# Gate and up products of a feed-forward layer by one level of Strassen's algorithm, with the down product in a stage of its own

## The chip, the core and the metric

The kernel runs on one core of a Trainium2 chip. The core has a matrix engine (TensorE, "PE" in the profile, its weight loads "PEld"), three engines for elementwise work (VectorE "DVE", ScalarE "ACT", GpSimd "POOL") and an engine that issues transfers between DRAM and the on-chip memory SBUF (SyncE, "SP"). PE writes its sums into PSUM, a small memory of eight banks. Each engine works through its own list of instructions in order and waits on semaphores for the others. The metric is the device time of one execution in microseconds (us). The kernel before was timed three times: median 2945.67 us, from 2942.64 to 2949.52.

## The reference, cut to what matters

A layer of a recurrent decoder is computed for 2112 tokens (64 sample tokens and 2048 prompt tokens), width 1024. A mixer with two kinds of recurrent heads comes first, then a residual and a LayerNorm give `x`. The part that matters here follows, with 2816 hidden features:

```python
hid = jax.nn.silu(x @ w_ffn_gate) * (x @ w_ffn_up)      # 1024 -> 2816, twice
f   = hid @ w_ffn_down                                  # 2816 -> 1024
y   = layer_norm(2 ** 0.25 * x + f, ln2_g, ln2_b)
```

All inputs are float32. The kernel computes each product of two float32 matrices by three matrix products: an operand `a` is split into a rounded part `h` and a rest `l = a - h` (the type `fp32r`), and `a b` is taken as `h_a h_b + h_a l_b + l_a h_b`.

## The kernel before, in words

The program has four stages, one after the other on the one core: the GLA heads, the GDN heads, the output projection with the first LayerNorm (`phase_out`), and the feed-forward part (`phase_ffn`). Tokens are handled in 17 units: unit 0 is the 64 sample tokens, units 1 to 16 are 128 prompt tokens each. The instructions of each engine are put in their order by a scheduler when the program is built; the order is fixed then, and within an engine nothing overtakes.

`phase_out` ends each unit in `project` (L1015) with the LayerNorm of `x` (`layer_norm`, L965), stores `x` to DRAM (`x1_d`, L1050), transposes it on PE (tiles `px`, L1056) and stores the transposed tiles as `x1T_d` (L1059).

`phase_ffn` (L1079) runs over three blocks of 704, 640 and 768 tokens (`fblocks`). For each block `load_x1` (L1089) brings in the transposed `x` as eight tiles of 128 features and splits each into `xh` (ACT, L1096) and `xl` (DVE, L128). Then it goes through the 22 groups of 128 hidden features `f`, taken one and then three at a time (`groups`). For each `f`:

- `load_gu` (L1101) loads a tile of gate weights and one of up weights, 128 by 1024 each; POOL casts the `h` part (L1107), DVE subtracts for the `l` part (L128).
- For each half of the block's tokens there are 24 matmuls into a PSUM tile `g` (gate) and 24 into a tile `u` (up), at L1144 to L1146. ACT applies SiLU to `g`, DVE multiplies with `u` (tile `sg`), and the result is split into `hh` (ACT, L1151) and `hl` (DVE). It stays in SBUF.
- `load_d` (L1112) loads and splits the down weights of this `f`.

After each group of `f`, the down products of all units of the block follow (L1169 to L1171, PSUM tile `dn`), and DVE adds their sums to the tile `y` in SBUF (L128, and L1173 for the first group). After the last group of a block comes the second LayerNorm and the store of the result.

`vtt` is an elementwise operation of two tensors on DVE (recorded as L128), `ptt` the same on POOL (recorded as L131). All transfers of this part, loads and stores, are issued by SP in one queue.

Of the kernel before, what the change touches and what calls it, by code (L numbers as in the profile page):

```python
# [9 lines left out]
F32 = mybir.dt.float32  # L10
# [8 lines left out]
D = 1024  # L19
# [4 lines left out]
DFF = 2816  # L24
# [76 lines left out]
def hybrid_layer(ctx: ExitStack, tc: tile.TileContext, I, O):  # L101
# [25 lines left out]
    def vtt(out, a, b, op):  # L127
        nc.vector.tensor_tensor(out, a, b, op=op)  # L128
# [19 lines left out]
    fblocks = [(0, 704, range(0, 6)), (704, 640, range(6, 11)), (1344, 768, range(11, 17))]  # L148
    x1T_d = [dram.tile([8, 128, T], F32, name=f"x1T_{i}") for i, (_, T, _) in enumerate(fblocks)]
# [836 lines left out]
    def phase_out(stack, main, rest):  # L986
# [28 lines left out]
        def project(u, gts):  # L1015
# [35 lines left out]
            fb = [i for i, f in enumerate(fblocks) if u in f[2]][0]  # L1051
            off = u0 - fblocks[fb][0]
            for i in range(2):
                pt = pmt("px").rearrange("p (h c) -> p h c", h=4)
                for h in range(4):
# [3 lines left out]
                ST.dma_start(out=x1T_d[fb][4 * i:4 * i + 4, :, off:off + C].rearrange("k p t -> p k t"),  # L1059
                             in_=t[:, :, :C])  # L1060
# [18 lines left out]
    def phase_ffn(stack):  # L1079
        pa = stack.enter_context(tc.tile_pool(reuse_waits=RW, name="pa", bufs=2))  # L1080
        NF = DFF // 128
        groups = [range(max(g, 0), g + 3) for g in range(NF % 3 - 3, NF, 3)]

        def split(pool, tag, bufs, shape):
            h = pool.tile(shape, F32R, name=tag + "h", tag=tag + "h", bufs=bufs)
            l = pool.tile(shape, F32R, name=tag + "l", tag=tag + "l", bufs=bufs)
            return h, l

        def load_x1(ib):  # L1089
            T = fblocks[ib][1]  # L1090
            xs = []
            for k in range(8):
                raw = pa.tile([128, 768], F32, name="xr")
                nc.sync.dma_start(out=raw[:, :T], in_=x1T_d[ib][k])
                h, l = split(pa, "x", 9, [128, 768])
                nc.scalar.copy(h[:, :T], raw[:, :T])  # L1096
                vtt(l[:, :T], raw[:, :T], h[:, :T].bitcast(F32), TT.subtract)
                xs.append((h, l))
            return xs

        def load_gu(f):  # L1101
            ws = []
            for n in ("w_gate", "w_upf"):
                raw = pa.tile([128, 8, 128], F32, name="wr")
                nc.sync.dma_start(out=raw, in_=I[n][:, 128 * f:128 * f + 128].rearrange("(k p) c -> p k c", p=128))
                h, l = split(pa, "w", 3, [128, 8, 128])
# [155 lines left out]
```

## Time and profile before

| | us |
|---|---|
| three timed runs, median (range) | 2945.67 (2942.64 to 2949.52) |
| the profiled execution, its own time | 2946.43 |
| span of that execution in the trace | 2944.4 |
| PE busy in the span | 2821.6 (96%) |
| DVE, ACT, POOL busy | 1425.6, 822.6, 515.6 |
| first matmul of the feed-forward part | starts at 1389.37 |
| mean granted PE clock | 0.974 of full speed |

A group's row in the profile reads: line, engine, operation, the program's names of output and inputs, their shapes, the count; then its busy time and the mean of one in ns; then the idle time of the engine before these instructions and what ended it. A row of the timeline reads: start in us, duration in us, engine, line, operation. Matmuls overlap: the next one starts before the end of the last, so that what a matmul costs is the distance from one start to the next and not its duration. A row of the windows gives for a stretch of time its length, the busy time of PE, PEld, DVE, ACT and POOL with the number of instructions, the granted PE clock, the busy share of the transfer engines and the rate in GB/s.

### The profile page before, as it was taken

Reading aid. Unit: us, or ns where it says so; the run is one execution under the profiler, and the core shown is the slowest. Engines: PE = TensorE matmul, PEld = TensorE weight load, DVE = VectorE, ACT = ScalarE, POOL = GpSimd, SP = SyncE. Lnnn points to the kernel's source line nnn. Section 1 sums busy time; section 2 is a strip of 40 time slices with the busy share of each in tenths; the row PEclk is TensorE's granted clock in tenths of the full one; section 3 lists DMA queues with packets and bytes.
Section 4 is the critical chain, followed back from the end, with each engine's and each line's share of the span. In section 5 each row is a group of like instructions: output and inputs, shape, how many; then the busy total and the mean of one; then the engine's idle time right before and its main releaser. Section 6 shows DMA issues by size and latency. Waiting matters only on the chain.

```text
span 2944.4 us, 43629 instructions
## 1 busy us (share of the span) xinstructions
PE 2821.6 (96%) x17686; PEld 2564.2 (87%) x17686; DVE 1425.6 (48%) x2428; ACT 822.6 (28%) x1852; POOL 515.6 (18%) x742
## 2 busy tenths in 40 slices
PE   7899996989998899999999999999999999999997
PEld 6799995878986788887999999999999999999996
DVE  4444453588897544445433333463333373333334
ACT  4243344376675433333211111111111121111111
POOL 2111111343343021111100000130010010000002
PEclk9899997799999999999999999999999999999998
DMA  5211134221213333334522222342222252222211
GB/s 152 62 59 37 51 99 68 71 69 37 67 49 85 122 123 101 115 101 150 182 65 70 67 65 65 103 156 77 78 73 79 79 170 65 64 62 62 64 44 45
DMA packets 291747, 246.62 MB, mean 84 GB/s; under 512 B 40672, under 2 KB 250896, under 8 KB 291536
## 3 DMA queue, kind: packets, MB, share of 16 engines
q1 hardware_dynamic: 289456, 243.64, 27.6%
q8 instruction: 141, 2.31, 0.3%
q14 instruction: 70, 0.57, 0.1%
q10 hardware_dynamic: 2080, 0.10, 0.0%
HBM read 201.03 MB, written 42.67 MB: 83 GB/s over the span
## 4 chain that ended last, share of the span: by engine, by line
PE 85%; DMA 5%; DVE 4%; ACT 2%; issue 2%; POOL 1%; SPq 0%; POOLq 0%; ACTq 0%; DVEq 0%
PE dn L1170 6%; PE dn L1171 6%; PE dn L1169 6%; PE u L1145 6%; PE u L1146 6%; PE u L1144 6%; PE g L1146 6%; PE g L1145 6%; PE g L1144 6%; PE g L205 3%; PE g L206 3%; PE g L207 3%; PE g L212 3%; PE g L213 3%; PE g L214 3%; PE pw L214 2%
## 5 line engine op out<-in xcount | busy, mean ns | idle before, releaser
L1107 POOL CAST wh<-wr 128x1024 fp32r<-128x1024 f32 x132 | 142.0, 1076 | 1289.0 <-PE g L1145 1096.7
L1144 PE MATMUL g<-xh,wh 128*128 128x352 f32 (+2 forms) x1056 | 340.5, 323 | 1.9 <-ACT xh L1096 1.9
L1145 PE MATMUL g<-xl,wh 128*128 128x352 f32 (+2 forms) x1056 | 341.0, 323 | 1.0 <-DVE xl L128 1.0
L1146 PE MATMUL g<-xh,wl 128*128 128x352 f32 (+2 forms) x1056 | 340.4, 323 | 0.0
L1146 PE MATMUL u<-xh,wl 128*128 128x352 f32 (+2 forms) x1056 | 340.1, 322 | 0.0
L1145 PE MATMUL u<-xl,wh 128*128 128x352 f32 (+2 forms) x1056 | 340.0, 322 | 0.0
L1144 PE MATMUL u<-xh,wh 128*128 128x352 f32 (+2 forms) x1056 | 340.0, 322 | 0.0
L1169 PE MATMUL dn<-dh,hh 128*128 128x512 f32 (+1 forms) x748 | 291.0, 390 | 2.5 <-ACT dh L1116 2.5
L1170 PE MATMUL dn<-dl,hh 128*128 128x512 f32 (+1 forms) x748 | 291.8, 390 | 0.0
L1171 PE MATMUL dn<-dh,hl 128*128 128x512 f32 (+1 forms) x748 | 291.2, 390 | 0.0
L128 DVE TENSOR_TENSOR sg<-sg,u 128x352 f32<-128x352 f32 (+2 forms) x132 | 68.7, 521 | 414.8 <-PE u L1146 413.1
L128 DVE TENSOR_TENSOR y<-y,dn 128x512 f32<-128x512 f32 (+1 forms) x238 | 162.6, 684 | 215.6 <-PE dn L1171 215.5
L128 DVE TENSOR_TENSOR wl<-wr,wh 128x1024 fp32r<-128x1024 f32 x132 | 169.2, 1282 | 123.5 <-POOL wh L1107 123.5
L225 DVE SCALAR_TENSOR_TENSOR cv<-hb,cw,cv 128x256 f32<-128x256 f32 x288 | 150.6, 531 | 112.5 <-ACT cv L223 107.7
L1144 PEld LDWEIGHTS g<-xh,wh 128*128 128x128 f32 x1056 | 198.5, 188 | 4.2 <-ACT xh L1096 2.6
L1145 PEld LDWEIGHTS g<-xl,wh 128*128 128x128 f32 x1056 | 198.6, 188 | 3.5 <-DVE xl L128 1.9
L1151 ACT CAST hh<-sg 128x352 fp32r<-128x352 f32 (+2 forms) x132 | 64.2, 487 | 490.6 <-DVE sg L128 490.5
L1146 PEld LDWEIGHTS g<-xh,wl 128*128 128x128 f32 x1056 | 198.9, 188 | 0.4
L1144 PEld LDWEIGHTS u<-xh,wh 128*128 128x128 f32 x1056 | 198.4, 188 | 0.3
L1145 PEld LDWEIGHTS u<-xl,wh 128*128 128x128 f32 x1056 | 198.3, 188 | 0.4
L1146 PEld LDWEIGHTS u<-xh,wl 128*128 128x128 f32 x1056 | 198.3, 188 | 0.1
L1116 ACT CAST dh<-dr 128x1024 fp32r<-128x1024 f32 x66 | 67.3, 1050 | 446.7 <-PE dn L1171 402.2
(321 smaller groups left out, 6274.3 us busy)
## 6 DMA issues: line engine op xcount, KB each, us to landing
wr<-in_w_gate SPq DMA_DIRECT2D x66, 512.0 KB, 3.8
wr<-in_w_upf SPq DMA_DIRECT2D x66, 512.0 KB, 3.7
dr<-in_w_down SPq DMA_DIRECT2D x66, 512.0 KB, 4.0
xraw<-in_xT SPq DMA_DIRECT2D x84, 256.0 KB, 3.2
on<-on SPq DMA_DIRECT2D x48, 256.0 KB, 3.6
wraw<-in_w_in SPq DMA_DIRECT2D x20, 512.0 KB, 4.0
xt<-in_x SPq DMA_DIRECT2D x16, 512.0 KB, 4.0
x<-xt SPq DMA_DIRECT2D x16, 512.0 KB, 3.6
```

Of the source, the lines that this page charges most:

```text
L128: nc.vector.tensor_tensor(out, a, b, op=op)
L205: nc.tensor.matmul(out, lhsT=wh[:, k, cs], rhs=xs[0][k], start=(k == 0), stop=False)
L206: nc.tensor.matmul(out, lhsT=wh[:, k, cs], rhs=xs[1][k], start=False, stop=False)
L214: nc.tensor.matmul(out, lhsT=xs[1][k][:, ts], rhs=wh[:, k, :], start=False, stop=(k == 7))
L225: nc.vector.scalar_tensor_tensor(dst, hb[:, i:i + 256], cw[:, f, i:i + 1], dst, op0=TT.mult, op1=TT.add)
L1107: nc.gpsimd.tensor_copy(h, raw)
L1144: nc.tensor.matmul(ps[:, :N], lhsT=h[:, k, :], rhs=xs[k][0][:, ts], start=(k == 0), stop=False)
L1145: nc.tensor.matmul(ps[:, :N], lhsT=h[:, k, :], rhs=xs[k][1][:, ts], start=False, stop=False)
L1146: nc.tensor.matmul(ps[:, :N], lhsT=l[:, k, :], rhs=xs[k][0][:, ts], start=False, stop=(k == 7))
L1169: nc.tensor.matmul(ps[:C], lhsT=hh[:, ts], rhs=wh[:, sl], start=first, stop=False)
L1170: nc.tensor.matmul(ps[:C], lhsT=hh[:, ts], rhs=wl[:, sl], start=False, stop=False)
L1171: nc.tensor.matmul(ps[:C], lhsT=hl[:, ts], rhs=wh[:, sl], start=False, stop=last)
```

## The change

Only the feed-forward part and what feeds it are changed.

**Gate and up together, seven products for eight.** The gate and up weights of one `f` are taken as one matrix of 256 outputs, the features of `x` in two halves of 512, and the tokens of a block in two halves of 352 (three equal blocks of 704). Written in these halves, gate and up are a 2 by 2 by 2 block product: eight block products of 12 matmuls each. One level of Strassen's algorithm (in Winograd's form) makes it seven, called by the right-hand operand: `11`, `S2`, `12`, `S1`, `S3`, `S4`, `22`. It needs four sums of halves of `x` per block (`sums`, on POOL; stored to DRAM in `xS_d` for blocks 1 and 2 and loaded again), four sums of quarters of the weights for each `f` in each block (`load_gu`, on POOL, in place of the casts that POOL did; the casts are ACT's now), and seven additions of the products for each `f` (on DVE, with one operand in PSUM). Each of the seven weight operands and seven `x` operands is split into `h` and `l` on ACT and DVE (`part`). A block product takes, for each of four tiles of 128 features, three matmuls with 352 tokens: 12 matmuls; one `f` has 84.

**The down product by itself.** SiLU times up is no longer split and kept, but stored to DRAM (`hid_d`) and loaded again after all three blocks are done. The down product then runs over five groups of units (4, 4, 3, 3, 3); the sums over all 22 `f` stay in the eight PSUM banks, and the down weights are loaded and split once per group, five times in all (three times before).

**Layout.** The weights come in an order that makes each load one contiguous piece per partition (`w_gu`, `w_dn`).

```diff
-    fblocks = [(0, 704, range(0, 6)), (704, 640, range(6, 11)), (1344, 768, range(11, 17))]
...
+    FT, FN = 704, 352
...
+    xS_d = [dram.tile([4, 4, 128, FN], F32, name=f"xS_{i}") for i in range(1, 3)]
+    hid_d = [dram.tile([128, NTOK], F32, name=f"hid_{f}") for f in range(DFF // 128)]
...
+        def part(pool, tag, bufs, shape, raw, N):
...
+            nc.scalar.copy(h[:, :N], raw)
+            vtt(l[:, :N], raw, h[:, :N].bitcast(F32), TT.subtract)
             return h, l
+        XO = ("11", "S2", "12", "S1", "S3", "S4", "22")
...
+        def raw_x():
+            return pa.tile([128, FN], F32, name="xr", bufs=8)
...
+        def sums(ib, k):
+            r = {n: load_raw(ib, n, k) for n in ("11", "21", "22", "12")}
+            r["S3"], r["S2"], r["S4"] = raw_x(), raw_x(), raw_x()
+            ptt(r["S3"], r["11"], r["21"], TT.subtract)
+            ptt(r["21"], r["21"], r["22"], TT.add)
+            r["S1"] = r["21"]
+            ptt(r["S2"], r["S1"], r["11"], TT.subtract)
+            ptt(r["S4"], r["12"], r["S2"], TT.subtract)
+            return r
         def load_x1(ib):
...
+            if ib == 0:
+                for k in range(4):
+                    r = sums(0, k)
+                    for n in XO:
+                        xs[n][k] = part(pa, "x", 28, [128, FN], r[n], FN)
+                return xs
+            for n in XO:
+                for k in range(4):
...
+                    xs[n][k] = part(pa, "x", 28, [128, FN], raw, FN)
...
+        x_first = load_x1(0)
+        yield
+        pw = stack.enter_context(tc.tile_pool(reuse_waits=RW, name="pw", bufs=2, side="right"))
...
+        psp = stack.enter_context(tc.tile_pool(reuse_waits=RW, name="psp", bufs=6, space=PSUM))
         def load_gu(f):
...
+            raw = pw.tile([128, 4, 512], F32, name="wr")
+            nc.sync.dma_start(out=raw, in_=I["w_gu"][f])
+            g1, g2, u2, u1 = (raw[:, i, :] for i in range(4))
+            t3, t2, t4 = (pw.tile([128, 512], F32, name="wt", bufs=3) for _ in range(3))
+            ptt(t3, u2, u1, TT.subtract)
+            ptt(u1, u1, g1, TT.subtract)
+            ptt(t2, u2, u1, TT.subtract)
+            ptt(t4, g2, t2, TT.subtract)
+            return {n: part(pw, "w", 9, [128, 512], r, 512)
+                    for n, r in zip(XO, (g1, t2, g2, u1, t3, u2, t4))}
...
+        for ib in range(3):
+            xs = load_x1(ib) if ib else x_first
+            for f in range(NF):
+                ws = load_gu(f)
+                def prod(n):
+                    (h, l), x = ws[n], xs[n]
+                    ps = psp.tile([128, 512], F32, name="p", tag="p")[:, :FN]
+                    for k in range(4):
...
+                g1, v, w, h1, h2 = (tmp() for _ in range(5))
+                nc.scalar.copy(g1, prod("11"))
+                vtt(v, g1, prod("S2"), TT.add)
+                vtt(g1, g1, prod("12"), TT.add)
+                act(g1, g1, AF.Silu)
+                vtt(w, v, prod("S1"), TT.add)
+                p = prod("S3")
+                vtt(v, v, p, TT.add)
+                vtt(h2, w, p, TT.add)
+                vtt(h1, w, prod("S4"), TT.add)
+                ptt(h1, h1, g1, TT.mult)
+                vtt(v, v, prod("22"), TT.add)
+                act(v, v, AF.Silu)
+                ptt(h2, h2, v, TT.mult)
+                for i, t in enumerate((h1, h2)):
...
+                    ST.dma_start(out=hid_d[f][:, t0:t0 + FN], in_=t)
+                if f == 10 and ib < 2:
+                    store_sums(ib + 1)
...
+        for nu in (4, 4, 3, 3, 3):
...
+            for f in range(NF):
+                if f % 2 == 0:
+                    raw = pw.tile([128, 4, 512], F32, name="wr")
+                    nc.sync.dma_start(out=raw, in_=I["w_dn"][f // 2])
+                wd = [part(pw, "w", 9, [128, 512], raw[:, 2 * (f % 2) + i, :], 512) for i in range(2)]
+                hr = p4.tile([128, 512], F32, name="hr")
+                nc.sync.dma_start(out=hr[:, :T], in_=hid_d[f][:, c0:c0 + T])
+                hh, hl = part(p4, "h", 3, [128, 512], hr[:, :T], T)
...
                     for u in us:
...
+            for u in us:
...
```

The scheduler gives the changed program the order that it now has. Up to the last projection of `phase_out` all engines have the same rows as before. Three places differ.

The first place is PE where the feed-forward part begins. `px` are the transposes of the last unit after its first LayerNorm. Before, the last projections (`pw`) are followed at once by gate and up products:

```order
L1146 MATMUL g_14875<-xh_14794,wl_14843 128x352
L1144 MATMUL g_14875<-xh_14800,wh_14842 128x352
L1145 MATMUL g_14875<-xl_14801,wh_14842 128x352
L1146 MATMUL g_14875<-xh_14800,wl_14843 128x352
L1146 MATMUL g_14930<-xh_14794,wl_14843 128x352
```

Now they are followed by the transposes, and then by the first product (`p_15045`, product `11` of the first `f`):

```order
L216 MATMUL pw_14761<-o1l_11567,oh_14729 128x512
L217 MATMUL pw_14761<-o1h_11590,ol_14730 128x512
L215 MATMUL pw_14761<-o1h_11590,oh_14729 128x512
L216 MATMUL pw_14761<-o1l_11591,oh_14729 128x512
L217 MATMUL pw_14761<-o1h_11590,ol_14730 128x512
L1057 MATMUL px_14797<-ident_60,xt_14733 128x128 x4
L1057 MATMUL px_14805<-ident_60,xt_14733 128x128 x4
L1179 MATMUL p_15045<-xh_14833,wh_15012 128x352
```

So the transposes of the last unit, which stood 44 matmuls behind the first gate product, now stand ahead of all products.

The second place is DVE within the gate and up products of one `f`. Before, in the third block (`sg` is the product with the up sums `u` in PSUM; `wl`, `hl` have both inputs in SBUF):

```order
L128 TENSOR_TENSOR wl_23858<-wr_23855,wh_23857 128x1024
L128 TENSOR_TENSOR sg_23663<-sg_23663,u_23638 128x384
L128 TENSOR_TENSOR hl_23612<-sg_23663,hh_23611 128x384
L128 TENSOR_TENSOR wl_23864<-wr_23861,wh_23863 128x1024
L128 TENSOR_TENSOR sg_23718<-sg_23718,u_23693 128x384
L128 TENSOR_TENSOR hl_23612<-sg_23718,hh_23611 128x384
```

Now, in the first block (`p` are products in PSUM, `t` their running sums, `wt` sums of weight quarters):

```order
L128 TENSOR_TENSOR wl_16340<-wt_16329,wh_16339 128x512
L128 TENSOR_TENSOR wl_16344<-wr_16326,wh_16343 128x512
L128 TENSOR_TENSOR t_16217<-t_16216,p_16235 128x352
L128 TENSOR_TENSOR wl_16348<-wr_16326,wh_16347 128x512
L128 TENSOR_TENSOR t_16216<-t_16216,p_16249 128x352
L128 TENSOR_TENSOR wl_16352<-wt_16328,wh_16351 128x512
L128 TENSOR_TENSOR t_16218<-t_16217,p_16264 128x352
L128 TENSOR_TENSOR wl_16356<-wr_16326,wh_16355 128x512
L128 TENSOR_TENSOR t_16217<-t_16217,p_16278 128x352
L128 TENSOR_TENSOR t_16220<-t_16218,p_16278 128x352
L128 TENSOR_TENSOR wl_16360<-wt_16330,wh_16359 128x512
L128 TENSOR_TENSOR t_16219<-t_16218,p_16293 128x352
```

Six instructions per `f` have become fourteen, and subtractions of weights for the next `f` alternate with additions that wait for the products of this one.

The third place is POOL in the same stretch. Before it had two casts per `f` and nothing else:

```order
L1107 CAST wh_15713<-wr_15711 128x1024
L1107 CAST wh_15719<-wr_15717 128x1024
L1107 CAST wh_15843<-wr_15841 128x1024
L1107 CAST wh_15849<-wr_15847 128x1024
L1107 CAST wh_16105<-wr_16103 128x1024
```

Now it has six operations of two tensors per `f`; in the first four `f` of blocks 0 and 1 the sums for the next block (`xr`) stand between them:

```order
L131 TENSOR_TENSOR t_15043<-t_15043,t_15040 128x352
L131 TENSOR_TENSOR t_15044<-t_15044,t_15041 128x352
L131 TENSOR_TENSOR wt_15446<-wr_15444 128x512
L131 TENSOR_TENSOR xr_16647<-xr_16639,xr_16641 128x352
L131 TENSOR_TENSOR wr_15444<-wr_15444 128x512
L131 TENSOR_TENSOR xr_16641<-xr_16641,xr_16643 128x352
L131 TENSOR_TENSOR xr_16648<-xr_16641,xr_16639 128x352
L131 TENSOR_TENSOR wt_15447<-wr_15444 128x512
L131 TENSOR_TENSOR xr_16649<-xr_16645,xr_16648 128x352
L131 TENSOR_TENSOR wt_15448<-wr_15444,wt_15447 128x512
```

A row such as `wt_15446<-wr_15444` reads two quarters of the same tile; the casts of the weights went from POOL to ACT.

More of the change, by code (lines that the diff above doesn't have):

```diff
@@ L1087, in split @@
             return h, l
-        def load_x1(ib):
[L1090 to L1098, printed above, removed]
-            return xs
@@ new lines, in store_sums @@
+        def store_sums(ib):
+            for k in range(4):
+                r = sums(ib, k)
+                for n in range(4):
+                    ST.dma_start(out=xS_d[ib - 1][n, k], in_=r[f"S{n + 1}"])
+        x_first = load_x1(0)
+        yield
+        pw = stack.enter_context(tc.tile_pool(reuse_waits=RW, name="pw", bufs=2, side="right"))
+        p4 = stack.enter_context(tc.tile_pool(reuse_waits=RW, name="p4", bufs=2, side="right"))
+        psp = stack.enter_context(tc.tile_pool(reuse_waits=RW, name="psp", bufs=6, space=PSUM))
@@ new lines, in phase_ffn @@
+        nc.sync.dma_start(out=lng, in_=I["ln"][2:3, :].to_broadcast([128, D]))
+        nc.sync.dma_start(out=lnb, in_=I["ln"][3:4, :].to_broadcast([128, D]))
+        n = 0
+        for nu in (4, 4, 3, 3, 3):
+            us = range(n, n + nu)
+            n += nu
+            c0, T = units[us[0]][0], sum(units[u][1] for u in us)
+            ps = {}
+            for u in us:
+                for i in range(2):
+                    ps[u, i] = (psg.tile([128, 512], F32, name="g", tag="g") if u == us[0] else
+                                psp.tile([128, 512], F32, name="p", tag="p"))
+            ys = {}
+            for f in range(NF):
[6 more added lines that the diff above has]
+                hh, hl = part(p4, "h", 3, [128, 512], hr[:, :T], T)
+                if f == 0:
@@ L1154, in phase_ffn @@
                     for u in us:
-                        ys[u] = p4.tile([128, D], F32, name="y", bufs=6)
+                        ys[u] = p4.tile([128, D], F32, name="y", bufs=5)
                         nc.sync.dma_start(out=ys[u][:units[u][1]], in_=x1_d[u])
-                    if ib == 0:
-                        nc.sync.dma_start(out=lng, in_=I["ln"][2:3, :].to_broadcast([128, D]))
-                        nc.sync.dma_start(out=lnb, in_=I["ln"][3:4, :].to_broadcast([128, D]))
                 for u in us:
@@ L1163, in phase_ffn @@
                     for i in range(2):
[L1164 to L1179 removed]
+                        p = ps[u, i][:C]
+                        nc.tensor.matmul(p, lhsT=hh[:, ts], rhs=wd[i][0], start=f == 0, stop=False)
+                        nc.tensor.matmul(p, lhsT=hh[:, ts], rhs=wd[i][1], start=False, stop=False)
+                        nc.tensor.matmul(p, lhsT=hl[:, ts], rhs=wd[i][0], start=False, stop=f == NF - 1)
+            for u in us:
+                u0, C = units[u]
+                for i in range(2):
+                    sl = slice(512 * i, 512 * i + 512)
+                    nc.vector.scalar_tensor_tensor(ys[u][:C, sl], ys[u][:C, sl], ALPHA, ps[u, i][:C],
+                                                   op0=TT.mult, op1=TT.add)
+                layer_norm(p4, ys[u], C, lng, lnb, spare=u < 16)
+                ST.dma_start(out=O["y"][u0:u0 + C, :], in_=ys[u][:C])
         yield
@@ L1224, in lay_out @@
     cst, msk = make_consts()
+    quads = lambda n, d: g(n)[512 * d:512 * d + 512].reshape(4, 128, 22, 128).transpose(2, 1, 0, 3)
     one, zero = np.ones(4, np.float32), np.zeros(4, np.float32)
```

102 lines of the change are left out of this document (31 added, 71 removed).

## Prediction

> **What bounds the kernel now.** I read the page first: busy times, and the span in 40 slices of 73.6 us.
>
> ```profile
> span 2944.4 us, 43629 instructions
> PE 2821.6 (96%) x17686; PEld 2564.2 (87%) x17686; DVE 1425.6 (48%) x2428; ACT 822.6 (28%) x1852; POOL 515.6 (18%) x742
> PE   7899996989998899999999999999999999999997
> PEclk9899997799999999999999999999999999999998
> ```
>
> The reader is to see that from slice 19 on, where the feed-forward part lies, PE is full and its clock is too. The windows give the ends of that part and a stretch within it:
>
> ```profile
> 1389.40:1416.00 26.60, 21.20 (x117) 19.07 (x115) 14.39 (x19) 7.25 (x12) 6.66 (x5) 0.94 0.85 244
> 1520.00:1620.00 100.00, 100.00 (x564) 92.48 (x563) 34.84 (x47) 11.62 (x21) 10.46 (x10) 1.00 0.23 69
> 2915.00:2944.00 29.00, 10.75 (x48) 8.58 (x46) 20.12 (x23) 3.03 (x3) 14.20 (x11) 0.74 0.24 94
> ```
>
> Within it DVE works a third of the time, ACT and POOL a tenth, the transfers a quarter: PE alone is the bound. So the part costs what its matmuls cost. Their groups give the counts (six groups like the first, three like the second), and the timeline gives the distance from start to start, first and last row of a run:
>
> ```profile
> L1144 PE MATMUL g<-xh,wh 128*128 128x352 f32 (+2 forms) x1056 | 340.5, 323 | 1.9 <-ACT xh L1096 1.9
> L1169 PE MATMUL dn<-dh,hh 128*128 128x512 f32 (+1 forms) x748 | 291.0, 390 | 2.5 <-ACT dh L1116 2.5
> ...
> 1506.50 0.32 PE L1144 MATMUL u<-xh,wh 128*128 128x352 f32 x1
> 1510.30 0.32 PE L1144 MATMUL g<-xh,wh 128*128 128x352 f32 x1
> ...
> 2099.83 0.31 PE L1144 MATMUL u<-xh,wh 128*128 128x320 f32 x1
> 2102.47 0.31 PE L1144 MATMUL g<-xh,wh 128*128 128x320 f32 x1
> ...
> 2884.47 0.33 PE L1144 MATMUL g<-xh,wh 128*128 128x384 f32 x1
> 2888.63 0.33 PE L1144 MATMUL u<-xh,wh 128*128 128x384 f32 x1
> ...
> 2110.01 0.39 PE L1169 MATMUL dn<-dh,hh 128*128 128x512 f32 x1
> 2115.91 0.39 PE L1171 MATMUL dn<-dh,hl 128*128 128x512 f32 x1
> ```
>
> The pairs are 24, 18, 24 and 26 matmuls apart: 0.1583, 0.1467, 0.1733 and 0.2269 us each. Gate and up are 6 x 1056 = 6336, a third in each block: 2112 x 0.4783 = 1010.2 us. Down is 3 x 748 = 2244: 509.2 us. Together 1519.4. The part runs from 1389.37 to the last matmul's end:
>
> ```profile
> 1389.37 0.33 PE L1144 MATMUL g<-xh,wh 128*128 128x352 f32 x1
> ...
> 2925.37 0.39 PE L1171 MATMUL dn<-dh,hl 128*128 128x512 f32 x1
> ```
>
> That is 1536.4 us, 17.0 above the matmuls. About 8 of these are the start (117 matmuls x 0.1583 = 18.5 in a stretch of 26.6).
>
> **What the change removes.** Gate and up become 3 blocks x 22 f x 84 = 5544 matmuls of 352 tokens: 877.6 us, 132.6 less. Down keeps its 2244. The floor of the part is 877.6 + 509.2 = 1386.8 us. All rows ahead of it are unchanged, and its end (second LayerNorm of the last units after the last matmul) is bound by DVE before and after: I put it at the same time. The question is what PE must now wait for.
>
> **Steady state: 13.30 us of PE per f.** Prices of the new rows:
>
> ```profile
> L128 DVE TENSOR_TENSOR xl<-xraw,xh 128x512 fp32r<-128x512 f32 x84 | 57.5, 693 | 16.9 <-ACT xh L195 16.8
> L128 DVE TENSOR_TENSOR sg<-sg,u 128x352 f32<-128x352 f32 x44 | 22.9, 521 | 116.6 <-PE u L1146 114.9 <-ACT sg L93 1.6
> L128 DVE TENSOR_TENSOR hl<-sg,hh 128x352 fp32r<-128x352 f32 x44 | 23.0, 523 | 19.9 <-ACT hh L1151 19.9
> L1038 ACT CAST oh<-pt 128x512 fp32r<-128x512 f32 x32 | 18.3, 579 | 11.5 <-PE pt L1035 11.5
> L93 ACT ACTIVATE sg<-g 128x352 f32<-128x352 f32 x44 | 20.4, 466 | 115.6 <-PE g L1146 115.6
> L131 POOL TENSOR_TENSOR y<-y,lnb 128x1024 f32<-128x1024 f32 x4 | 9.5, 2382 | 5.0 <-ACT y L976 3.8 <-ACTq L1196 1.3
> ```
>
> Per f, ACT has 7 x 0.579 + 3 x 0.466 = 5.45 us. DVE has 7 x 0.693 = 4.85 for the rests of the weights and 7 x 0.521 = 3.65 for the additions: 8.50. POOL has, by 2.382 us for 1024 columns, 4 x 1.191 + 2 x 0.819 = 6.40. Each alone fits in 13.30. But DVE and POOL get in each other's way, as the end of the trace shows:
>
> ```profile
> 2915.59 0.69 DVE L128 TENSOR_TENSOR y<-y,dn 128x512 f32<-128x512 f32 x1
> 2921.85 2.91 DVE L974 SCALAR_TENSOR_TENSOR y<-y,mv,lng 128x1024 f32<-128x1024 f32 x1
> 2932.84 1.28 DVE L974 SCALAR_TENSOR_TENSOR y<-y,mv,lng 128x1024 f32<-128x1024 f32 x1
> ...
> 2915.81 2.40 POOL L131 TENSOR_TENSOR y<-y,lnb 128x1024 f32<-128x1024 f32 x1 [1.26 <-ACT y L976]
> 2921.29 2.39 POOL L131 TENSOR_TENSOR y<-y,lnb 128x1024 f32<-128x1024 f32 x1 [1.26 <-ACT y L976]
> ```
>
> The operation of 1.28 us took 2.91 when it began under POOL's: POOL ended at 2923.68, and 2923.68 + 1.08 is its end. It stood still until POOL was done. The addition that reads PSUM took its 0.69 us with POOL's beside it. So POOL's 6.40 and the 4.85 us of weight rests exclude each other, 11.25 of 13.30 per f, while the 3.65 of additions may lie under POOL's. PE keeps the pace, with 2.05 us per f to spare.
>
> The Trainium skill has a rule for this (SBUF — State Buffer, Who interferes with whom): VectorE and GpSimd share one port pair, held for a whole instruction, and a VectorE instruction contends with a GpSimd one that reads SBUF only where it has two SBUF inputs. It speaks against a change that gives POOL six such instructions for two casts; by it the steady state is the 11.25 above and no bound, and if instead every DVE instruction stood still it would be 8.50 + 6.40 = 14.90. The trace agrees with the rule: 0.69 for the PSUM addition, 2.91 for the one with two SBUF inputs.
>
> Bounds for the wait in steady state: 0, and 14.90 - 13.30 = 1.60 per f if no addition lies under POOL's. Weights are split up to nine products ahead and six PSUM tiles take up lags, so I am near the lower end: 0.25 per f, 66 x 0.25 = 16 us.
>
> **Transfers and SP's queue.** Per f SP now issues one load of 1 MB and two stores of `hid`, 176 KB each, for three loads of 512 KB: 106 GB/s where the windows show 69 now and 244 at the start. The new wait is that of the stores for POOL's last product; behind them stands the load of weights for three f later, whose buffer comes free only in mid-f anyway, and after landing (3.8 us for 512 KB, below; some 6 for 1 MB) it is used nearly an f later. I take nothing; if this cover were gone, a late load would cost its lateness once per f. The way of `hid` through DRAM has hundreds of us. ACT's casts hide behind PE with 5.45 of 13.30.
>
> **The start.** Before, PE went straight from projections to gate products. Now the last unit's transposes stand ahead of all products, and each tile of the seven operands needs `x` parts of all four k. Rows of before at that place:
>
> ```profile
> 1375.41 1.15 SPq L1094 DMA_DIRECT2D xr<-x1T  x2
> 1399.60 1.28 DVE L979 SCALAR_TENSOR_TENSOR xt<-xt,mv,lnb 128x1024 f32<-128x1024 f32 x1
> 1400.90 0.32 SPq L1050 DMA_DIRECT2D x<-xt  x1
> ...
> xr<-x1T SPq DMA_DIRECT2D x8, 352.0 KB, 3.8
> wr<-in_w_gate SPq DMA_DIRECT2D x66, 512.0 KB, 3.8
> ```
>
> Loads begin at 1375.4 again. There are eight buffers `xr`, and one k takes seven (four loads, three sums), so the four k follow each other: a load of 3.8 us, then four sums on POOL and seven rests on DVE, which exclude each other: 4 x 0.819 + 7 x 0.523 = 6.9; some of both overlaps with the neighbours, I take 8 us per k. Three k end at 1399.4; the last unit's LayerNorm on DVE comes in between, 5 us, and so do the first weights (7 x 0.693 on DVE, 4 x 1.191 on POOL, 9.6 in all, some 4 of them ahead of the last k's second operand). 1399.4 + 5 + 4 = 1408.4, and half of the last k gives about 1414 for the second product; six products of 12 x 0.1583 = 1.90 end f 0 at 1425.5. Without waits it would have ended at 1389.4 + 13.3 = 1402.7: a loss of 23 us. Bounds: 8 as before, and 40 if nothing overlaps.
>
> **Seams between blocks.** A block brings 28 rests of `x` on DVE, 28 x 0.523 = 14.6, and, for the next one, 16 sums on POOL, 16 x 0.819 = 13.1, in the first four f of blocks 0 and 1. The spare 2.05 us per f takes part of it. Block 0: 13.1 - 4 x 2.05 = 4.9. Block 1: rests and sums over about six f, 27.7 - 12.3 = 15.4. Block 2: 14.6 - 2 x 2.05 = 10.5. Together 30.8; between 0 (the buffers cover all) and 55.4 (they cover nothing).
>
> **Down.** Per f and group of three units PE has 18 x 0.2269 = 4.08 us; DVE has 3 x 0.693 = 2.1, ACT 1.7. All eight banks are in use, so a new group waits for additions out of PSUM (eight of the 0.69 us above), but DVE begins them with the first unit while PE still works on the others: 0 to 5.5 per start, I take 1.5, five times 7 us. What replaces the additions of partial sums is less work for DVE, hidden either way.
>
> **Sum.** 1386.8 + 16 + 23 + 30.8 + 7 = 1463.6 against 1536.4: 72.8 less. The profiled execution took 2946.43, 0.8 above the median of the three; 2946.4 - 72.8 = 2873.6, forecast 2874.
>
> **Rivals.**
>
> *The shared access sets the pace; slower.* If DVE stands still for all of POOL's operations, f takes 14.90, and nothing is spare for the seams: 1386.8 + 105.6 + 23 + 55.4 + 7 = 1577.8, 41 more than before: 2988. For it: both engines work in order, and a blocked rest holds up the addition behind it. Against it: half the rows of DVE between two rests are additions that read PSUM. It costs from the point where more than 4.80 of POOL's 6.40 us per f hold DVE up, and makes the kernel slower from about 5.8.
>
> *The buffers cover all seams.* Only the start remains: 1386.8 + 23 = 1409.8, time 2820. For it: weights nine products ahead are 17 us. Against it: the parts of the next `x` have no buffers of their own, they wait for the products of the last f.
>
> *The down stage waits for transfers.* In groups of three each f moves 512 KB of weights and 192 KB of `hid` in 4.08 us, 177 GB/s; the window at the start shows 244 GB/s at a share of 0.85. If only 150 came, each of these 66 f would take 4.81: 48 us more than the forecast, 2922.
>
> That the change doesn't do what it says I leave out: the order has 84 matmuls per f.
>
> **Chances.** Forecast 0.60 (its own range 2840 to 2915), covered seams 0.10, transfers 0.08, shared access 0.14 (all of it slower), other losses at the seams that leave a gain 0.08. No change is what lies within 0.2%, about what a measurement here can tell: 2940 to 2951, 0.03 between the cases. Faster 0.83, slower 0.14. The range leaves out the better half of the covered seams and most of the shared access: 2825 to 2965.
>
> **What would show it.** Products 1.90 us apart in mid-block, and f 13.3 to 13.6 us apart, show the steady state right; 14.5 or more, with PE waiting for DVE there, show the shared access. A second product before 1405 or after 1425 shows the start wrong. Gaps of PE at both block seams should sum to some 25 us and more at the first. Down steps of 5.4 and 4.1 us without gaps show that stage right. I am wrong if PE waits in mid-block.

## The result, and the profile after the change

The changed kernel takes 2866.74 us (median of four runs, 2859.88 to 2881.43), 0.9731 of the kernel before, with a 95% interval of 0.9688 to 0.9775: faster. Its profiled execution took 2869.59 us, against 2946.43 before: 76.8 less.

The first rows and the slices of the page of the changed kernel (40 slices of 71.7 us):

```profile
span 2867.8 us, 45407 instructions
PE 2712.7 (95%) x16894; PEld 2438.8 (85%) x16894; DVE 1795.6 (63%) x3030; ACT 1202.6 (42%) x2584; POOL 989.0 (34%) x1066
...
PE   7899996889998899999799999999999999999996
POOL 2111121343433121111686558655665500211111
```

PE is as full as before, with 792 matmuls less. What grew is the work beside it: POOL from 515.6 to 989.0 us, DVE from 1425.6 to 1795.6. The windows of the changed kernel show where that lies: the start, a stretch of gate and up, all of down, and what follows the last matmul (columns: length; busy time and count of PE, PEld, DVE, ACT, POOL; clock of PE; share of the DMA engines; GB/s):

```profile
1389.40:1408.70 19.30, 6.87 (x31) 5.51 (x30) 17.25 (x26) 7.98 (x20) 14.40 (x13) 0.72 0.71 242
1408.70:1440.00 31.30, 22.36 (x111) 21.33 (x110) 29.36 (x32) 14.28 (x29) 27.16 (x19) 0.79 0.69 230
1500.00:1600.00 100.00, 100.00 (x627) 100.00 (x626) 78.85 (x110) 43.04 (x78) 61.56 (x47) 1.00 0.33 109
...
2319.80:2845.50 525.70, 524.85 (x2246) 414.02 (x2244) 273.98 (x410) 185.85 (x334) 59.98 (x44) 1.00 0.51 174
2845.50:2867.80 22.30, 0.00 (x0) 0.00 (x0) 11.14 (x14) 2.30 (x2) 9.28 (x8) 0.57 0.19 75
```

In mid-block PE is busy for all of 100 us: 627 matmuls touch this window, and over the whole stage they are 0.1600 apart from start to start, 13.44 us per `f`. The waits of PE over the rest of gate and up, from the end of `f` 0 on, and those of the start (columns: us in total, times, longest):

```profile
PE p L1180 <- DVE xl L128: 3.2, 3, 1.3
PE p L1179 <- DVE t L128: 2.5, 1, 2.5
PE p L1179 <- ACT xh L1097: 1.0, 2, 0.8
```

```profile
PE px L1057 <- DVE xt L982: 12.4, 1, 12.4
PE p L1180 <- DVE xl L128: 5.6, 1, 5.6
PE p L1181 <- DVE wl L128: 1.8, 1, 1.8
PE p L1179 <- ACT xh L1097: 1.5, 1, 1.5
```

So 880 us of gate and up hold under 7 us of waits, and the first 42 us hold 21. The timeline gives the marks of the stages: the last projection matmul, the first matmul of `f` 1, of down, and the last one.

```profile
1394.32 0.40 PE L217 MATMUL pw<-o1h,ol 128*128 128x512 f32 x1
...
1436.02 0.32 PE L1179 MATMUL p<-xh,wh 128*128 128x352 f32 x1
...
2319.85 0.39 PE L1237 MATMUL g<-wh,hh 128*64 128x512 f32 x1
...
2845.07 0.39 PE L1239 MATMUL p<-wh,hl 128*128 128x512 f32 x1
```

Before, the last projection matmul began at 1389.13; here it began 5.2 us later. The first output projection matmul, at 1018.08 for 1012.89 before, was already as late, long ahead of the first changed row, so this is scatter between executions. Against the prediction's terms, counted from that matmul on:

| term | predicted | measured |
|---|---|---|
| gate and up, matmuls alone | 877.6 | 887.0 (66 x 13.44) |
| steady state, waits | 16 | 0 |
| start | 23 | 28.0 (1436.0 - 1394.6 - 13.4) |
| seams | 30.8 | 10.2 (2319.85 - 1436.02 - 65 x 13.44) |
| down, matmuls alone | 509.2 | 523.7 (2244 x 0.2334) |
| down, starts of groups | 7 | 1.9 |
| sum | 1463.6 | 1450.8 |
| part ahead of it | as before | 5.2 later |
| after the last matmul | as before, 18.6 | 22.3 |

The time was forecast to 0.3%, but by terms that were off by 4 to 21 us in both directions. The experiments ask which of them stand.

### The profile page after: what moved, and what is told of

It is laid out like the page before. It is cut to its first block, busy times and chain, and to the rows that moved or that the text cites. A ratio compares the mean times of both kernels' runs of the same rounds, so it can differ in the third digit from the quotient of the medians.

```text
span 2867.8 us, 45407 instructions
## 1 busy us (share of the span) xinstructions
PE 2712.7 (95%) x16894; PEld 2438.8 (85%) x16894; DVE 1795.6 (63%) x3030; ACT 1202.6 (42%) x2584; POOL 989.0 (34%) x1066
## 4 chain that ended last, share of the span: by engine, by line
PE 79%; DMA 7%; DVE 5%; ACT 3%; issue 3%; POOL 2%; SPq 0%; POOLq 0%; ACTq 0%; DVEq 0%
PE p L1180 10%; PE p L1181 10%; PE p L1179 10%; PE p L1237 4%; PE p L1239 4%; PE p L1238 4%; PE g L216 3%; PE g L215 3%; PE g L217 3%; PE g L208 3%; PE g L209 3%; PE g L210 3%; PE pw L217 2%; PE pw L215 2%; PE pw L216 2%
## 5 line engine op out<-in xcount | busy, mean ns | idle before, releaser
L128 DVE TENSOR_TENSOR wl<-wr,wh 128x512 fp32r<-128x512 f32 x484 | 466.5, 967 | 289.5 <-ACT wh L1097 286.7
L1180 PE MATMUL p<-xl,wh 128*128 128x352 f32 x1848 | 599.2, 324 | 8.8 <-DVE xl L128 8.8
L1179 PE MATMUL p<-xh,wh 128*128 128x352 f32 x1848 | 598.0, 324 | 5.1 <-ACT xh L1097 2.6
L1181 PE MATMUL p<-xh,wl 128*128 128x352 f32 x1848 | 598.2, 324 | 1.8 <-DVE wl L128 1.8
L1097 ACT CAST wh<-wr 128x512 fp32r<-128x512 f32 x484 | 298.1, 619 | 474.4 <-PE p L1239 259.5
L1180 PEld LDWEIGHTS p<-xl,wh 128*128 128x128 f32 x1848 | 349.2, 189 | 10.4 <-DVE xl L128 10.0
L1179 PEld LDWEIGHTS p<-xh,wh 128*128 128x128 f32 x1848 | 348.7, 189 | 6.2 <-ACT xh L1097 3.4
L1181 PEld LDWEIGHTS p<-xh,wl 128*128 128x128 f32 x1848 | 349.1, 189 | 2.2 <-DVE wl L128 2.2
L128 DVE TENSOR_TENSOR t<-t,p 128x352 f32<-128x352 f32 x462 | 232.9, 516 | 108.7 <-PE p L1181 107.1
L1237 PE MATMUL p<-wh,hh 128*128 128x512 f32 x528 | 208.8, 395 | 0.0
L208 PE MATMUL g<-xh,wAh 128*128 128x256 f32 (+1 forms) x512 | 154.0, 302 | 16.7 <-ACT hs L232 16.1
## 6 DMA issues: line engine op xcount, KB each, us to landing
wraw<-in_w_in SPq DMA_DIRECT2D x20, 512.0 KB, 3.8
```

The lines of the kernel that those rows point to most:

```text
L208: nc.tensor.matmul(out, lhsT=wh[:, k, cs], rhs=xs[0][k], start=(k == 0), stop=False)
L1097: nc.scalar.copy(h[:, :N], raw)
L1179: nc.tensor.matmul(ps, lhsT=h[:, ks], rhs=x[k][0], start=k == 0, stop=False)
L1180: nc.tensor.matmul(ps, lhsT=h[:, ks], rhs=x[k][1], start=False, stop=False)
L1181: nc.tensor.matmul(ps, lhsT=l[:, ks], rhs=x[k][0], start=False, stop=k == 3)
L1237: nc.tensor.matmul(p, lhsT=hh[:, ts], rhs=wd[i][0], start=f == 0, stop=False)
```

## The experiments

Except where a median is given, a kernel was timed once and is read by its stages: the part ahead of the feed-forward, which no edit touches, ended between 1374.9 and 1396.9 us in these runs, so single whole times tell nothing below some 20 us. This table has, for each run, the time from the last projection matmul to the end of `f` 0 (A), from there to the first matmul of down (B), down (C), and what follows the last matmul (D), in us:

| run | A | B | A + B | C | D |
|---|---|---|---|---|---|
| the changed kernel | 41.7 | 883.8 | 925.5 | 525.6 | 22.3 |
| eight products | 44.2 | 1006.0 | 1050.2 | 525.2 | 22.4 |
| two of three matmuls | 37.5 | 780.5 | 818.0 | 525.0 | 24.1 |
| sums of weights doubled | 38.5 | 1037.6 | 1076.0 | 524.4 | 22.6 |
| wider weight tiles | 40.8 | 893.5 | 934.2 | 526.7 | 22.4 |
| seven weight buffers | 40.6 | 884.3 | 924.9 | 527.8 | 22.2 |
| four weight buffers | 35.0 | 891.8 | 926.7 | 535.2 | 23.0 |
| fourteen `xr` | 42.8 | 897.3 | 940.1 | 530.5 | 22.5 |
| sums of `x` on DVE | 44.8 | 883.6 | 928.4 | 530.1 | 22.5 |
| gap of 64 bytes | 42.4 | 884.9 | 927.3 | 513.4 | 22.6 |
| staggered end | 41.9 | 879.6 | 921.5 | 525.7 | 19.5 |
| gap and staggered end | 42.3 | 881.1 | 923.4 | 511.9 | 19.7 |
| the same, weights held back | 36.2 | 888.0 | 924.2 | 512.0 | 19.3 |

**Eight products instead of seven.**

```diff
-                    for k in range(4):
+                    turns = [(r, k) for r in range(2 if n == "22" else 1) for k in range(4)]
+                    for r, k in turns:
```

> The seventh product (22) of every f is computed twice into the same bank, so PE has the eight products of the ordinary algorithm while every other engine, every transfer and the down stage stay as they are. Theory (PE alone sets the pace of gate and up, the saving is the matmuls left out): 66 x 12 more matmuls at 0.160 us = 127 us more, less what is left of gaps at the seams (up to 9): 2988 to 2997 us, that is slower than before the change. Rival (another engine sets the pace, or the gain comes from the new down stage): clearly less than 100 us more than the 2869.6 of the change's profiled run.

(The value of that product doubles.) Measured: 2996.45 us, 126.9 more than the changed kernel; A + B is 124.7 longer. The saving is the matmuls left out, all of them on the path. With eight products the new arrangement takes 1597.8 us from the last projection matmul to the end (A + B + C + D), where the kernel before takes 2944.4 - 1389.1 = 1555.3: 42.5 us are the price of the sums, the new start, the slower down stage and the longer end, and Strassen's 127 us pay it.

**What the other engines could do, and what they do when POOL has more.**

```diff
-                        nc.tensor.matmul(ps, lhsT=h[:, ks], rhs=x[k][0], start=k == 0, stop=False)
-                        nc.tensor.matmul(ps, lhsT=h[:, ks], rhs=x[k][1], start=False, stop=False)
+                        nc.tensor.matmul(ps, lhsT=h[:, ks], rhs=x[k][1], start=k == 0, stop=False)
```

> The first of the three matmuls of every k (xh with wh) is left out of gate and up, so PE needs only 56 x 0.160 = 9.0 us per f and the other engines must show their own pace; the output is not the reference's. Theory (weight rests on DVE and sums on POOL exclude each other, additions from PSUM do not): f lies between 11.25 (4.85 + 6.40) and the 13.3 that the changed kernel reaches without gaps, about 12; the whole 66 x (12 - 13.6) = 105 less, about 2765 us. Rival (no exclusion): PE's 9.0 to 9.8 per f, some 250 less, about 2600. Rival (DVE stands still for all of POOL's work): no less than 14.9, no gain at all.

```diff
             ptt(t4, g2, t2, TT.subtract)
+            ptt(t3, u2, t2, TT.subtract)
+            ptt(t4, g2, t2, TT.subtract)
+            ptt(t3, u2, t2, TT.subtract)
+            ptt(t4, g2, t2, TT.subtract)
```

> POOL computes four more sums of 128x512 per f (two operands then have other values; the output is not the reference's). POOL alone would have 6.40 + 4 x 1.19 = 11.2 us per f, under PE's 13.3. Theory (exclusion of rests and sums): 11.25 + 4.77 = 16.0 per f, 2.7 more than PE's, 66 x 2.7 = 178 more: about 3050 us, with gaps of PE waiting for DVE's rests in mid-block. Rival (the engines do not hold each other up much, POOL has its own time): under 20 us more.

A window in the last block of each, first with two of three matmuls, then with the doubled sums (columns as above):

```profile
2090.00:2180.00 90.00, 78.85 (x440) 69.56 (x440) 88.72 (x111) 39.27 (x78) 65.59 (x48) 1.00 0.36 126
```

```profile
2300.00:2400.00 100.00, 93.89 (x557) 88.84 (x557) 78.90 (x94) 33.47 (x66) 97.57 (x67) 1.00 0.26 89
```

With two of three the whole took 2760.25 us, and A + B is 107.5 shorter, where 105 had been expected. In the window stand 440 matmuls, 56 per `f`, in 90 us: 11.5 us per `f`, with DVE busy 99% of the time, though the durations of its operations without company would add up to 8.5. That is the prediction's 11.25, where rests and sums exclude each other; without exclusion PE would have kept 9.0, and where all of DVE stands still 14.9 would have come. With the sums doubled, 557 matmuls, 84 per `f`, in 100 us: 15.1 per `f`, POOL busy 98%, where the theory has 16.0 and POOL alone 11.2. A + B grew by 150.5, not 178, and not as the theory had it: the pace of 15.1 accounts for some 110, since the changed kernel's own `f` is 13.4 and not 13.30 and 15.1 is less than 16.0. Most of the rest stands at the block starts, whose first `f` take 30.9 and 30.6 us where nothing is spare to cover them. The exclusion holds to within some 0.9 us per `f`, and the changed kernel has 1.9 us per `f` to spare. The Trainium skill states such an exclusion for two SBUF inputs (SBUF — State Buffer, Who interferes with whom); these two rows agree with it. The two-port modes of copies and casts, which the same section adds, don't arise here: all of DVE's rows in these windows are operations of two tensors.

**What covers the seams.**

```diff
-            return {n: part(pw, "w", 9, [128, 512], r, 512)
+            return {n: part(pw, "w", 7, [128, 512], r, 512)
```

> Seven buffers for weight parts (and two products less of lead) instead of nine. Theory (at the block seams the rests of x and the sums for the next block are covered by the weight parts that stand ready, not by spare time of DVE and POOL): with less lead the gaps of PE between f 1 and the end of gate and up grow from about 9 us to 20 or 30, and the whole by 10 to 25 us over the 2869.6 of the change's profiled run. Rival (the spare time alone covers them): the gaps stay within 3 us of what they are.

> Four buffers for weight parts instead of nine: a lead of at most four products (7.7 us). With seven the seams did not grow. Theory (what covers the seams is the lead of the parts of weights and x over PE): with four, the 14.6 us of rests of x per block can hide behind at most 7.7 and the spare 1.9 per f (13.4 less the 11.5 that f took where PE did not set the pace): gaps of 5 us or more at each of the two block starts, and 8 to 20 us in all over the 8 of the changed kernel. Rival (spare time alone): gaps stay at 8 to 11 us.

The second has a 4 in the place of the 7. With seven, B is 0.5 longer, where gaps 11 to 21 longer had been expected: two buffers less do nothing. With four it is 8.0 longer, and the first `f` of blocks 1 and 2 take 19.2 and 18.8 us where the changed kernel has 16.7 and 14.6: gaps of 5.7 and 5.3, as the theory said (14.6 less 7.7 and 1.9 is 5.0). In the run with two of three matmuls, where PE leaves little lead to build up, the same two take 26.4 and 27.8 against its 11.5, 14.9 and 16.3 more: about the 14.6 us of rests of `x`, uncovered. (C of the second run is longer because these buffers serve down too: PE waits there 6.8 us for rests of weights.) So what covers a seam is work done ahead, by more than four products and not more than seven. How much of it is lead of weights and how much lead of `x` itself was not tried apart.

**The start.** First more buffers for `x`:

```diff
-            return pa.tile([128, FN], F32, name="xr", bufs=8)
+            return pa.tile([128, FN], F32, name="xr", bufs=14)
```

> Fourteen buffers xr instead of eight, so that the loads of the next k need not wait for the parts of the last (room for them: the pool of x is closed before down, and the buffers hr, h and y of down come into its place). From the last projection's matmul to the end of f 0 it takes 41.6 us in the changed kernel. Theory (the four k follow each other because of the buffers): about 10 us less, the whole 8 to 12 less. Rival (the sums on POOL and the rests on DVE hold each other up there, and the weights of f 0 with them): under 3 us less.

The theory falls: A is no shorter. B is 13.5 longer. Half of that has nothing to do with `x`: to make room, this kernel puts down's buffers in the place of those of `x`, so the first hidden parts are loaded only after the last product, and the first matmul of down waits for them (us in total, times, longest):

```profile
PE g L1240 <- ACT hh L1098: 6.5, 1, 6.5
```

The rest is in the first two `f` of blocks 1 and 2 (16.8 and 19.2, 14.6 and 20.1 us, for 16.7 and 14.9, 14.6 and 13.4), less 4.3 that `f` 4 of block 0 gains; that rests of `x`, loaded earlier, now push weights and additions back on DVE is only argued. Then the sums of block 0 on DVE:

```diff
-            ptt(r["S3"], r["11"], r["21"], TT.subtract)
+            stt = ptt if ib else vtt
+            stt(r["S3"], r["11"], r["21"], TT.subtract)
```

(and so for the other three.)

> The 16 sums of x for block 0 are made by DVE (0.52 us each) instead of POOL (0.82); those of blocks 1 and 2 stay on POOL. Since fourteen buffers did not shorten the start, the theory is now: between 1384 and 1424 rests on DVE and sums on POOL have the shared access to themselves in turn, 16 x 0.82 + 28 x 0.52 + 4 x 1.19 + 7 x 0.69 = 37.3 us, which is the distance itself. With the sums on DVE it is 16 x 0.30 = 4.8 less, and no operation waits there for POOL's: f 0 ends 4 to 10 us earlier (41.9 us after the last projection's matmul now). Rival (what sets the start is the last unit's LayerNorm, which stands between these operations on DVE, or the loads): under 2 us, or later.

That falls too: A is 3.1 longer. What the runs before had not asked is in which order DVE works. Its timeline in the changed kernel, with PE's around its longest wait for a product:

```profile
1409.95 1.42 DVE L128 TENSOR_TENSOR wl<-wr,wh 128x512 fp32r<-128x512 f32 x1
1411.29 1.60 DVE L128 TENSOR_TENSOR xl<-xr,xh 128x352 fp32r<-128x352 f32 x1
1412.81 1.43 DVE L128 TENSOR_TENSOR wl<-wt,wh 128x512 fp32r<-128x512 f32 x1
1414.17 2.37 DVE L128 TENSOR_TENSOR wl<-wr,wh 128x512 fp32r<-128x512 f32 x2
...
1420.81 1.75 DVE L128 TENSOR_TENSOR wl<-wr,wh 128x512 fp32r<-128x512 f32 x1
1422.48 3.76 DVE L128 TENSOR_TENSOR xl<-xr,xh 128x352 fp32r<-128x352 f32 x6
...
1417.89 0.59 PE L1179 MATMUL p<-xh,wh 128*128 128x352 f32 x2 [1.55 <-ACT xh L1097]
1424.12 0.66 PE L1180 MATMUL p<-xl,wh 128*128 128x352 f32 x1 [5.64 <-DVE xl L128]
```

Eight rests of weights stand between 1409.95 and 1422.48 ahead of the last six of the last `k`'s rests of `x`. PE had use for the first two alone by then (products `11` and `S2`), and it waits for the first of those six. With four buffers DVE can't run so far ahead, and A was 6.7 shorter. Another kernel holds back five of the nine buffers, for `f` 0 of block 0 alone (on top of the two edits below):

```diff
+                if late and n == "S3":
+                    for m in late:
+                        nc.scalar.copy(pw.tile([128, 512], F32R, name="wh", tag="wh", bufs=9)[:, :8],
+                                       x_first[m][3][1][:, :8].bitcast(F32))
+                    late.clear()
                 ws[n] = part(pw, "w", 9, [128, 512], r, 512)
...
+        late = list(XO[-5:])
```

> In addition five of the nine buffers for weight parts are held back once, in f 0 of block 0 only, until the x parts of the last k are made: on DVE four rests of weights, not nine, then stand ahead of the last six rests of x; later f have all nine. Theory (the start was long because nine rests of weights stood in DVE's queue ahead of the last k of x: with four buffers throughout, f 0 ended 35.0 us after the last projection's matmul instead of 41.9): f 0 ends at 35 to 37 us after it and the seams stay at 8 to 11 us; the whole 5 to 7 under the other kernel of this pair. Rival (the early end with four buffers came from something else, for example fewer transfers): 41 to 42 as before, no gain.

DVE's timeline at that place in that run:

```profile
1416.15 2.37 DVE L128 TENSOR_TENSOR wl<-wr,wh 128x512 fp32r<-128x512 f32 x2
1419.87 3.88 DVE L128 TENSOR_TENSOR xl<-xr,xh 128x352 fp32r<-128x352 f32 x4 [1.35 <-ACT xh L1097]
1423.97 0.96 DVE L128 TENSOR_TENSOR xl<-xr,xh 128x352 fp32r<-128x352 f32 x2 [0.22 <-ACT xh L1097]
```

A is 36.2 instead of 42.3: the order in DVE's queue did set the length of the start. But B is 6.9 longer, 5.1 of it in `f` 2 to 4 (14.5, 15.4 and 15.4 us for 13.4), where PE now waits for additions of DVE, and A + B is 924.2 against 923.4; the time is 2849.56 against 2850.8, no difference. Most of what PE no longer waits for at the start it waits for two `f` later. A + B lies between 921.5 and 928.4 in eight of ten runs with seven products and single sums, however it divides, and never below: moving work between DVE and POOL and among their first `f` gained nothing. That part of the expectation, 5 to 7 us less in all, fell.

**Down: where the operands lie.** One kernel makes the tiles of weight parts wider, so that each begins at another place:

```diff
-            return {n: part(pw, "w", 9, [128, 512], r, 512)
+            return {n: part(pw, "w", 9, [128, 552], r, 512)
```

> The tiles of weight parts are 552 columns wide instead of 512 (the first 512 used), so that the nine buffers start at different places (160 bytes apart modulo 2 KB); the buffers y of the down stage are four instead of five to make room. Theory A (the slower pace of down, 0.2333 us a matmul against 0.2271 before, comes from where the moving rows begin): some buffers show 0.227 and others 0.233 or more, a mean between. Theory B (it comes from changing the PSUM bank after every three matmuls, or from the place of the stationary operand): 0.233 for all buffers. The whole changes by less than 13 us either way.

Its matmuls of down came 0.2317 apart on the mean (0.231 is the median), between the 0.2271 of before and the 0.2333 after, with no clear order by buffer: neither theory holds as put, and all that it shows is that changing places alone moved the pace. The other shifts all hidden parts by 64 bytes:

```diff
+        gap = stack.enter_context(tc.tile_pool(reuse_waits=RW, name="gap", bufs=1, side="right"))
+        nc.gpsimd.memset(gap.tile([128, 16], F32, name="gap"), 0.0)
         p4 = stack.enter_context(tc.tile_pool(reuse_waits=RW, name="p4", bufs=2, side="right"))
```

> A gap of 64 bytes between two pools moves the hidden parts (the stationary operand of down) so that they begin at the same place modulo 128 bytes as the weight rows that stream past them; nothing else changes. In the runs so far 512-wide products took 0.227 us where the two places were equal modulo 128 (down before, the gate projections) and 0.233 where they were 64 apart (down after, the output projections). Theory (the relative place matters): 0.227 in the whole down stage, 525.6 us become about 511, the whole 13 less. Rival (chance, something else differs): 0.233 as before, no change. The run with shifted weight tiles, a mean of 0.2311 with no clear order by place, speaks for the rival.

The first and the last of ten matmuls in a row of the changed kernel, then of eleven, and the two ends of the stage, in the shifted one:

```profile
2499.73 0.40 PE L1237 MATMUL g<-wh,hh 128*128 128x512 f32 x1
...
2501.84 0.39 PE L1237 MATMUL p<-wh,hh 128*128 128x512 f32 x1
```

```profile
2499.72 0.39 PE L1239 MATMUL p<-wh,hh 128*128 128x512 f32 x1
...
2501.99 0.39 PE L1240 MATMUL p<-wl,hh 128*128 128x512 f32 x1
...
2314.97 0.40 PE L1239 MATMUL g<-wh,hh 128*64 128x512 f32 x1
...
2827.98 0.39 PE L1241 MATMUL p<-wh,hl 128*128 128x512 f32 x1
```

2.11 us for nine distances, 2.27 for ten: 0.234 and 0.227. The stage takes 513.4 us instead of 525.6. The theory holds; the rival, drawn from the run with wider tiles, does not. There every matmul had another place than the next, and the pace of each seems to depend on more than its own.

**The end.** In each group the last two `f` are done unit by unit:

```diff
+                have = [(f, wd, hh, hl)] if f != NF - 1 else [*have, (f, wd, hh, hl)]
+                if f == NF - 2:
+                    continue
                 for u in us:
                     u0, C = units[u]
                     ts = slice(u0 - c0, u0 - c0 + C)
+                    for fe, we, he, le in have:
```

> In each group of down the last two f are done unit by unit instead of f by f, so the units end 12 matmuls (2.8 us) apart and DVE can begin with the first while PE works for the others. Theory (the end of the program became longer, 22.3 us against 18.6 before, because three units end together): 3 to 5 us less after the last matmul, and the gaps of PE between groups (about 1.5 us) go. Rival (the last unit's own chain sets the end): under 1 us.

19.5 us after the last matmul instead of 22.3, just under the range that the theory gave. The gaps of PE between groups did not go: C is 525.7 for 525.6. The changed kernel's timeline shows what follows its last matmul:

```profile
2845.07 0.39 PE L1239 MATMUL p<-wh,hl 128*128 128x512 f32 x1
2850.74 2.34 POOL L131 TENSOR_TENSOR y<-y,lnb 128x1024 f32<-128x1024 f32 x1 [2.71 <-ACT y L979]
2853.04 2.38 POOL L975 TENSOR_SCALAR mv<-mv 128x1 f32<-128x1 f32 x2
2850.84 4.51 DVE L977 SCALAR_TENSOR_TENSOR y<-y,mv,lng 128x1024 f32<-128x1024 f32 x2
```

All three units end with PE, and their steps get in one another's way: POOL's addition for one unit (2.34) stands in its queue ahead of the `mv` of the other two, and two of DVE's normalizations, 1.28 us each, take 4.51 because the first stands still for that addition. Before, one of DVE's stood still in the same way (2.91 for 1.28), so how the 3.7 us divide among these was not shown. B of this run is 4.2 shorter, without an edit there; other pairs of runs whose gate and up are alike differ by as much (881.1 and 884.9 with the gap), so nothing is read into it.

**Together.**

> The gap of 64 bytes and the staggered end together. If the two gains are independent (12.2 us in the down stage, 2.8 after the last matmul), the whole is 15 less than the changed kernel's 2866.7: about 2852, 0.968 of the kernel before. If the one depended on the order of the other (the last two f unit by unit lose the even places of operands): the down stage is back over 520 us.

2850.8 us (median of five, 2844.72 to 2853.73), 0.9668 of the kernel before, 0.9644 to 0.9691: faster. It was not run beside the changed one, but every run of it is shorter than any of those; by the medians it is 15.9 less, by the stages C and D 13.7 and 2.6 less. The two gains add up.

## Why the prediction was right, and where not

**The saving and its steady state: right in mechanism.** PE sets the pace of gate and up, an `f` takes 13.4 us, and the engines beside it could do 11.5 where 11.25 was worked out. Of the three accounts of the shared access, the one taken (rests and sums exclude each other, additions from PSUM do not) is the one that both pressure runs bear out; the rival of 14.90 per `f` is excluded, and the bound that put 16 us here was not needed at all.

**The floor was low by 9.4.** The step "24 matmuls apart: 0.1583" took a short run of rows. The 352-wide matmuls of the changed kernel came 0.1600 apart over the whole stage, and those of the kernel before 0.1607: the mean over a stage, not two rows of it, was the price to take.

**The start was mis-sized, 23 for 28.0.** The sum hides two errors of opposite sign. The second product began at 1414.52, as worked out (1414), but by luck: this execution was 5.2 us late from its first loads of `x` on (1380.61 for 1375.41), so that it was due at 1419 and came 4.7 early. From there to the end of `f` 0 it took 21.5 us for the 11.4 that had been put, because PE stood for the last `k`, 1.55 and 5.64 us: the step "some 4 of them ahead of the last k's second operand" counted too few rests of weights in DVE's queue. Nor had the sum a term for the clock: from 1424.57 on the matmuls come 0.293 apart instead of 0.160, for some 4 us.

```profile
1380.61 2.16 SPq L1110 DMA_DIRECT2D xr<-x1T  x4
...
1414.52 0.49 PE L1179 MATMUL p<-xh,wh 128*128 128x352 f32 x1
...
1424.57 0.49 PE L1181 MATMUL p<-xh,wl 128*128 128x352 f32 x1
...
1427.80 0.49 PE L1181 MATMUL p<-xh,wl 128*128 128x352 f32 x1
```

**The seams were mis-sized, 30.8 for 10.2.** By block it was 4.3, 4.7 and 1.2 for 4.9, 15.4 and 10.5: the block with sums alone came out as worked out, and those with rests of `x` did not. The step took only the spare time of the `f` in which the work stands (1.9 per `f`, 2.05 predicted) against them. What was done ahead in the `f` before covers most of the rest, as the gaps with four buffers show. Of the rival that buffers cover all, most came true. Start and seams were priced apart, but they are one account: 38.2 measured against 53.8.

**Down was mis-sized, 516.2 for 525.6.** The step that "down keeps its 2244" at 0.2269 carried a duration over to operands that lie elsewhere. The starts of groups cost 1.9, not 7.

**Transfers: the rival fell.** Down moved 174 GB/s, and PE was idle in it for less than 1 us. Loads of 1 MB landed in 4.9 us by the page, where 6 had been taken.

**The end: "the same" was wrong by 3.7.** The groups finish all their units at once; before, one unit after the other. Finishing them one by one gave 2.8 of it back.

The errors (+9.4 floor, -16 steady state, +5.0 start, -20.6 seams, +9.4 down, +5.2 ahead of the part, +3.7 at the end) add up to -3.9: the forecast of 2873.6 and the profiled 2869.6 agree because they cancel, and that is luck.

## What to carry to other kernels

Where two engines exclude each other, add up their exclusive work against the engine that sets the pace, and treat a start and the seams after it as one account: what one stage is spared by a better order, the next may pay. A duration holds for its operands where they lie: after moving a stage to new tiles, compare the distance from matmul to matmul with the old one before looking for waits. And a deep prefetch fills an in-order queue at the start with work that is not due yet.

## What the runs showed of the hardware

**512-wide fp32r matmuls had two paces, and the relative place of their operands decided.** The places are those of the tiles in SBUF, in bytes modulo 128, as the built programs have them; the pace is the distance from start to start over the stage:

| matmuls | streamed | stationary | apart (streamed less stationary) | ns |
|---|---|---|---|---|
| down, before | 32 | 32 | 0 | 227 |
| gate projections | 0 | 0 | 0 | 227 |
| down, with the gap (three runs) | 96 | 96 | 0 | 227 |
| output projections | 64 | 0 | 64 | 233 |
| down, after (and with 7 or 4 buffers) | 96 | 32 | 64 | 233 |
| down, with fourteen `xr` | 96 | 0 | 96 | 233 |

No absolute place is fast or slow by itself: 96 and 32 stand in both halves. The 352-wide matmuls show nothing of the kind: 0.1607 before, at equal places, 0.1600 after, 32 apart, 0.1607 with the wider tiles, where all four distances occur. Why it is so no run here shows, nor what 32 apart does to 512-wide ones by itself: with the wider tiles that distance alternates with the other three. The Trainium skill (TensorE: Matmul & The Clock Gate, Back-to-back issue gap) gives for an isolated matmul the columns over 2.4 GHz and about 2.5 ns, which makes an estimate of 215.8 ns here, and about 131 ns for a sustained stream of 512-wide ones; both paces measured are longer, and the measurement decides.

**A wait of PE costs more than itself.** After the wait of 5.6 us in `f` 0 the matmuls came 0.293 apart for about 4 us, and then 0.160 again. The windows of these two stretches and of one behind a wait of 2.5 us, in `f` 4 of block 0, give the granted clock (the column behind POOL's):

```profile
1424.60:1428.30 3.70, 3.70 (x14) 3.70 (x14) 3.70 (x8) 0.88 (x2) 1.33 (x1) 0.50 1.01 311
1428.80:1436.00 7.20, 7.20 (x47) 7.20 (x46) 6.98 (x10) 2.36 (x4) 7.12 (x6) 1.00 0.97 352
1486.70:1490.00 3.30, 3.27 (x11) 3.30 (x12) 3.15 (x5) 2.35 (x5) 2.53 (x3) 0.50 0.40 151
```

The Trainium skill (the same page, What's actually happening) describes a clock that is halved after an idle stretch of some 3.4 us until the engine has been busy for as long; the rows agree in kind, but in this trace a wait of 2.5 us was enough.
